# A four-layer mixer trunk on one core: fewer bias copies, norm rows two slots apart, spatial mixes in the other PSUM pool, first transfers reordered

## The chip, the cores and the metric

The program runs on one core of one Trainium2 chip. The metric is the device time of one execution in microseconds (us); the time before is the median of three runs. Four engines compute: TensorE (PE in the profile; its weight loads are PEld), VectorE (DVE), ScalarE (ACT) and GpSimd (POOL). SyncE (SP) only issues transfers here. Each engine works through its own queue in order, and an instruction that waits holds up everything behind it on that engine. Transfers (DMAs) are issued from the queues of SP, ACT and POOL and are carried out by 16 DMA engines that they share.

## What is computed

The reference is a trunk of four layers over 256 tokens of width 2048, in float32. Every layer normalises the stream, multiplies it by one wide input projection, runs a mixer over 1536 columns and an attention over 256 memory tokens over the other 512, gates the result and projects it back:

```python
mem_n = rms_norm(mem, mem_norm_g)
for i in range(4):
    h = rms_norm(x, norm_g[i])
    z = h @ w_in                      # mixer inputs | memory queries | gate
    # layers 0 and 3: gated spatial mixing, layer 1: forgetting attention,
    # layer 2: differential attention with a relative position bias
    mix_out = mixer(z[..., :n_mix])
    kv = mem_n @ w_mem_kv[i]
    mem_out = memory_attention(rms_norm(z_q), rms_norm(kv[..., :512]), kv[..., 512:])
    x = x + (concatenate([mix_out, mem_out]) * silu(gate)) @ w_out[i]
```

Two parts matter for the change. The spatial mixing of layers 0 and 3 multiplies 128 tokens at a time by a 128 x 128 matrix for each of 12 channel groups. The differential attention of layer 2 adds to the scores of each of its 12 heads a bias that depends only on the distance of key and query: `bias = table[t5_bucket(kpos - qpos)]`. So a row of 383 numbers per head holds all of it, and each query's row of 256 is a window of that row, one place further along than the next query's.

## The kernel before

**Products in slots.** All weights, some 300 MB, are read once from device memory, in pieces of 512 KB (128 partitions x 1024 float32). A piece is one slot: SP loads it into a `raw` buffer (line 105), ACT rounds it into `whi` (line 118), DVE subtracts to get the rest `wlo` (line 119), and PE does 12 matmuls of 128x512 with it, three products for each of two halves and two token tiles (lines 185 to 187). The three products together stand for one product in more exact arithmetic. Eight slots make a chunk of 512 output columns. There are 592 slots. Four `raw` buffers and four pairs `whi`/`wlo` let the splitting run up to four slots ahead of PE, and the loads up to eight.

**Tasks between slots.** The order of PE, ACT, DVE and SP is written out by hand. Everything that is not a slot is a Python generator, a task. Before each slot every live task runs up to its next `yield` (a tick), then the splits and loads for later slots are emitted, then what tasks put off (`late`). So a `yield` more moves a task's rest one slot back in all four queues, against the slots. A task that is spawned runs its first part at once, and its second part two ticks later. POOL's order is not written by hand: a planner places POOL's instructions, so that one can be placed well ahead of where the text of the program has it.

**The parts that the change touches.**

- The start (lines 251 to 277): the gains `gk`, the first piece of the transposed memory (`raw`, tile `xraw`) and the first weights (`w_raw`) are loaded in halves from the queues of ACT and SP, and ten matmuls on zeros run meanwhile.
- `token_rms` (line 295) loads 256 token rows in four column blocks of two tiles each (line 308), lets ACT square and sum them two steps later (line 301), and at its end computes the factors `r_mem` or `r_x`. Its tiles come from a rotation of six buffers, tag `mo`. It runs twice: for the memory from the seventh tick on during the first 16 slots, and for `x` during the keys of the last memory projection. One step takes one tick.
- `norm_task` (line 377) normalises queries or keys of a chunk: squares on ACT, sums on DVE, a power on POOL (line 335, reads DVE's sums), scaling on DVE (line 349), a byte shuffle on ACT (line 359) and two DMA transposes on SP (line 364), a join on DVE (line 369), a gain on ACT (line 393), then `done()`, for which the attention waits.
- `gmlp_mix_task` (line 717) is the spatial mix; its result `sv` is a PSUM tile of pool `ps_s` (line 730). `ps_s` has two buffers and also serves the scores `s` of all attentions (line 509); `ps_t`, two buffers too, serves the attentions' transposes and products `tb` (line 595).
- `diff_setup` (line 469) computes the 12 bias rows on PE near the end of layer 0 and writes them to device memory (`bias_d`) in 128 copies, with a pitch of 513, in eight writes of 16 copies each (line 492, on POOL's queue). `bias_load` (line 496) reads the bias of four heads into SBUF with a single transfer of 128 partitions, each from another copy (line 502, POOL's queue). With that pitch a partition finds its shifted window at a constant step of 512. Layer 2 loads three such biases into a rotation of two buffers: two at its start, the third when the first chunk's attention has ended.

In layers 0 to 2 `residual_task` (line 833) adds the output chunk to the stream, stores it (`x_d`, POOL's queue), squares it, turns it with two DMA transposes (`xq`, line 364, by way of the helper `turn`), joins the halves on DVE (`wide`, line 369) and splits it for the next layer.

Of the kernel before, what the change touches and what calls it, by code (L numbers as in the profile page):

```python
# [20 lines left out]
P = 128  # L21
D = 2048
S = 256
# [7 lines left out]
BIG = 3.0e38  # L31
BIAS_PITCH = 512
RAW_BUFS = 4
PART_BUFS = 4
# [8 lines left out]
def trunk_kernel(  # L43
# [213 lines left out]
    bparts[0] = (m_hi, m_lo)  # L257
    nc.scalar.dma_start(gk, gk_in)
    nc.scalar.dma_start(raw[:, :S], mem_t[0, :, :S])
    nc.sync.dma_start(w_raw[:, :CW], pieces[0][0][0, :, :CW])  # L260
    nc.sync.dma_start(raw[:, S:], mem_t[0, :, S:])
    nc.sync.dma_start(w_raw[:, CW:], pieces[0][0][0, :, CW:])
# [32 lines left out]
    def token_rms(src, r):  # L295
        ss = small.tile([P, 2, 4], F32, tag="ss", name="ss", bufs=2)
        rows = {}
        for n in range(6):
            if n >= 2:
                for t, row in enumerate(rows.pop(n - 2)):  # L300
                    nc.scalar.activation(
                        row, row, AF.Square, accum_out=ss[:, t, n - 2 : n - 1]
                    )
            if n < 4:
                rows[n] = []
                for t in range(2):
                    row = tmp.tile([P, CW], F32, tag="mo", name="row", bufs=6)
                    nc.sync.dma_start(
                        row, src[t * P : (t + 1) * P, n * CW : (n + 1) * CW]
                    )  # L310
                    rows[n].append(row)
            if n < 5:
                yield
        late.append(lambda: finish_rms(ss, r))
# [62 lines left out]
    def norm_task(acc, rcols, gain, width, dst, done=None):  # L377
# [15 lines left out]
        nc.scalar.activation(dst, dst, AF.Copy, scale=gain)  # L393
        yield
        if done:
            done()
# [18 lines left out]
    spawn(load_transposed(mem_t, "b", 4 * KT, bparts, early, 1, 2))  # L415
    spawn(delayed(6, token_rms(mem, r_mem)))
    first_accs = pair_product(lambda kp: bparts[kp])
# [46 lines left out]
    nc.gpsimd.dma_start(onehot, onehot_in)  # L464
    bias_row = P * (BIAS_PITCH + 1)
    bias_d = dram.tile([NH, bias_row], F32, name="bias_d")


    def diff_setup():
# [14 lines left out]
        bd = bias_d[:, :]  # L484
        for a in range(0, P, 16):
            for _ in range(4):
                yield
            rows = bass.AP(
                tensor=bd.tensor, offset=bd.offset + a * (BIAS_PITCH + 1),
                ap=[[bias_row, NH], [BIAS_PITCH + 1, 16], [1, 384]],  # L490
            )
            nc.gpsimd.dma_start(
                rows, onehot[:NH].unsqueeze(1).to_broadcast([NH, 16, 384])
            )

    def bias_load(dst, c):
        bd = bias_d[:, :]
        src = bass.AP(
            tensor=bd.tensor, offset=bd.offset + 4 * c * bias_row + P - 1,
            ap=[[BIAS_PITCH, P], [bias_row, 4], [1, S]],  # L500
        )
        nc.gpsimd.dma_start(dst, src)

# [213 lines left out]
    def gmlp_mix_task(acc, rcols, v, ws, c, j, mos, flag):  # L717
# [11 lines left out]
        for t in range(2):  # L729
            sv = ps_s.tile([P, CW], F32, tag="s", name="sv")  # L730
            mo = tmp.tile([P, CW], F32, tag="mo", name="mo", bufs=6)
# [148 lines left out]
    for i in range(DEPTH):  # L880
# [65 lines left out]
        else:  # L946
# [3 lines left out]
            if kind == 1:  # L950
                cq = act.tile([P, 2, NH], F32, tag="cq", name="cq")
            else:
                for c in range(2):
                    bias_load(biases[c], c)
                fflag.append(True)
            width = HD if kind == 1 else HD // 2
            gq, gkc = (G_BQ, G_BK) if kind == 1 else (G_CQ, G_CK)
            for c in range(3):
# [18 lines left out]
                def finish(mo, c=c):  # L977
                    mos[c] = mo
                    if c == 0:
                        biases[2] = new_bias()  # L980
                        (cum_load if kind == 1 else bias_load)(biases[2], 2)

# [114 lines left out]
```

## Time and profile before

| | |
|---|---|
| runs | median 1751.71 us, 1748.94 to 1752.92 (3 runs) |
| profiled execution | 1753.51 us, its span from first to last instruction 1751.7 us |
| busy share of the span | PE 99%, DVE 61%, ACT 56%, POOL 7% |
| moved | 381.13 MB, mean 218 GB/s |
| mean granted TensorE clock | 0.997 |

The span is cut into views: the waits list who waited for whom in total, the windows give busy time and the number of instructions (x) of each engine in a stretch, with the granted clock (PEclk, 1.00 is full) and the share of DMA engine time in use; the timeline has each instruction's start, duration, engine, line and in brackets how long its engine sat idle before it and what ended that. A busy share of 99% does not say that PE runs at its full rate: ends of matmuls are modelled and a matmul's time counts as busy however slowly the next one follows. The number of matmuls in a window says more.

### The profile page before, as it was taken

How to read it: one execution, taken by the hardware profiler on the slowest of the kernel's cores; microseconds unless marked ns; L12 is line 12 of the kernel's file. 1: busy time of each engine (PE TensorE's matmuls, PEld its weight loads, DVE VectorE, ACT ScalarE, POOL GpSimd, SP SyncE). 2: the span in 40 equal slices, each digit the busy share in tenths (PEclk: the TensorE clock that was granted, in tenths of full speed). 3: DMA queues.
4: the chain of work that ended last, by engine and by line, in shares of the span. 5: the costliest groups of instructions: out<-in, count | busy, mean ns of one | idle time of the engine just before them, and what ended most of it. 6: DMA issues, size and time to landing. Idle time of an engine off the chain costs nothing.

```text
span 1751.7 us, 21860 instructions
## 1 busy us (share of the span) xinstructions
PE 1733.1 (99%) x7918; PEld 1424.9 (81%) x7918; DVE 1075.2 (61%) x1539; ACT 981.6 (56%) x1347; POOL 124.5 (7%) x142
## 2 busy tenths in 40 slices
PE   9999999999999999999999999999999999999999
PEld 7888787888778888888888888878888888888887
DVE  5656557565556656666666666767576656755553
ACT  6555645555555655565655665665575554555542
POOL 1111101000000100000000101101000000100000
PEclk9999999999999999999999999999999999999999
DMA  8888867577898666676688776666668887656774
GB/s 299 270 248 269 264 224 209 166 214 178 244 254 265 187 181 213 193 201 207 190 252 256 240 193 203 183 182 196 196 182 251 263 244 231 181 174 197 205 237 161
DMA packets 207260, 381.13 MB, mean 218 GB/s; under 512 B 113796, under 2 KB 116240, under 8 KB 207152
## 3 DMA queue, kind: packets, MB, share of 16 engines
q1 hardware_dynamic: 199440, 358.01, 68.6%
q0 software_dynamic: 6272, 20.50, 4.2%
q8 instruction: 62, 1.02, 0.2%
q10 hardware_dynamic: 1440, 1.22, 0.2%
q14 instruction: 46, 0.38, 0.1%
HBM read 339.55 MB, written 14.95 MB: 202 GB/s over the span
## 4 chain that ended last, share of the span: by engine, by line
PE 90%; DMA 6%; ACT 2%; DVE 1%; issue 1%; SPq 0%; POOL 0%; ACTq 0%; DVEq 0%; POOLq 0%
PE acc L185 28%; PE acc L186 28%; PE acc L187 28%; PE tb L602 2%; DMA raw<-in_w_o_dram 1%; ACT whi L118 1%; DMA xraw<-in_mem_t_dram 1%; PE tb L611 1%; DMA sq<-pl 1%; DVE wlo L119 1%; DMA xraw<-in_x_t_dram 1%; PE s L510 1%; PE s L552 1%; DMA xq<-pl 1%; PE sv L734 1%
## 5 line engine op out<-in xcount | busy, mean ns | idle before, releaser
L119 DVE TENSOR_TENSOR wlo<-raw,whi 128x1024 fp32r<-128x1024 f32 x591 | 719.3, 1223 | 487.3 <-ACT whi L118 482.4
L118 ACT CAST whi<-raw 128x1024 fp32r<-128x1024 f32 x591 | 616.6, 1050 | 460.5 <-PE acc L187 339.2
L185 PE MATMUL acc<-whi,xh 128*128 128x512 f32 x1600 | 637.3, 398 | 0.0
L187 PE MATMUL acc<-whi,xl 128*128 128x512 f32 x1600 | 623.9, 390 | 0.0
L186 PE MATMUL acc<-wlo,xh 128*128 128x512 f32 x1600 | 623.6, 390 | 0.0
L185 PEld LDWEIGHTS acc<-whi,xh 128*128 128x128 f32 x1600 | 300.5, 188 | 67.3 <-issue 4.2
L187 PEld LDWEIGHTS acc<-whi,xl 128*128 128x128 f32 x1600 | 300.3, 188 | 63.8
L186 PEld LDWEIGHTS acc<-wlo,xh 128*128 128x128 f32 x1600 | 300.7, 188 | 59.8
L185 PE MATMUL acc<-whi,bh 128*128 128x512 f32 x764 | 299.7, 392 | 7.3 <-ACT whi L118 5.9
L186 PE MATMUL acc<-wlo,bh 128*128 128x512 f32 x764 | 299.9, 393 | 3.5 <-DVE wlo L119 3.3
L187 PE MATMUL acc<-whi,bl 128*128 128x512 f32 x764 | 299.0, 391 | 0.0
L185 PEld LDWEIGHTS acc<-whi,bh 128*128 128x128 f32 x764 | 144.4, 189 | 39.4 <-ACT whi L118 6.7
L186 PEld LDWEIGHTS acc<-wlo,bh 128*128 128x128 f32 x764 | 144.4, 189 | 37.2 <-DVE wlo L119 6.8
L187 PEld LDWEIGHTS acc<-whi,bl 128*128 128x128 f32 x764 | 144.3, 189 | 30.1 <-DVE bl L221 0.2
L615 ACT COPY pt<-tb 128x256 f32<-128x256 f32 (+1 forms) x80 | 27.3, 341 | 126.9 <-PE tb L611 126.9
L335 POOL TENSOR_TENSOR sc<-sc,expo 128x8 f32<-128x8 f32 (+1 forms) x23 | 58.3, 2533 | 426.0 <-DVE sc L334 265.2
L359 ACT COPY pl<-sq 128x1024 uint16<-128x1024 uint16 x40 | 39.8, 1043 | 5.8 <-DVE sq L349 5.7
L220 ACT ACTIVATE xh<-wide,gk 128x256 fp32r<-128x256 f32 x48 | 20.5, 498 | 39.6 <-DVE wide L369 39.6
L369 DVE COPY wide<-xq 128x1024 uint16<-128x1024 uint16 x24 | 18.1, 754 | 36.7 <-DMA xq<-pl 36.2
L848 POOL DMA_DIRECT2D x_d<-xo x24 | 13.3, 554 | 326.6 <-DVE xo L847 326.1
L359 ACT COPY pl<-mo 128x1024 uint16<-128x1024 uint16 x32 | 31.9, 1044 | 7.7 <-DVE mo L658 7.6
L515 DVE TENSOR_REDUCE st<-s 128x1 f32<-128x256 f32 x32 | 13.5, 421 | 30.4 <-PE s L510 30.3
(170 smaller groups left out, 994.5 us busy)
## 6 DMA issues: line engine op xcount, KB each, us to landing
raw<-in_w_a_dram SPq DMA_DIRECT2D x176, 512.0 KB, 4.3
raw<-in_w_o_dram SPq DMA_DIRECT2D x128, 512.0 KB, 4.4
raw<-in_w_b_dram SPq DMA_DIRECT2D x112, 512.0 KB, 4.2
raw<-in_w_c_dram SPq DMA_DIRECT2D x112, 512.0 KB, 4.1
raw<-in_w_kv_dram SPq DMA_DIRECT2D x63, 512.0 KB, 4.9
x_d<-xo POOLq DMA_DIRECT2D x24, 256.0 KB, 6.1
xo<-x_d SPq DMA_DIRECT2D x24, 256.0 KB, 5.7
lnp<-in_ln_dram SPq DMA_DIRECT2D x12, 256.0 KB, 6.0
```

The source lines that it names most:

```text
L118: nc.scalar.copy(hi, raw)
L119: nc.vector.tensor_sub(lo, raw, hi.bitcast(F32))
L185: nc.tensor.matmul(acc[t], xh[:, c], wh, start=begin, stop=False)
L186: nc.tensor.matmul(acc[t], xh[:, c], wl, start=False, stop=False)
L187: nc.tensor.matmul(acc[t], xl[:, c], wh, start=False, stop=end)
L220: nc.scalar.activation(hi, src, AF.Copy, scale=g)
L335: nc.gpsimd.tensor_tensor(sc[:, :, :n], sc[:, :, :n], expo.rearrange("p (a b) -> p a b", a=2)[:, :, :n], ALU.pow,)
L359: nc.scalar.copy(pl.rearrange("p (h e) -> p h e", h=2), src.bitcast(U16).rearrange("p (e h) -> p h e", h=2),)
L369: nc.vector.tensor_copy(wide[:, :, t, :].bitcast(U16).rearrange("p c (r h) -> p h c r", h=2), tts[t].rearrange("p (h c) r -> p h c r", h=2),)
L510: nc.tensor.matmul(s[:, :S], qt[:, h, t * P : (t + 1) * P], mk[:, h * S : (h + 1) * S], start=True, stop=True,)
L602: nc.tensor.matmul(av, pt[:, j * P : (j + 1) * P], vv[:, j, f], start=(j == 0), stop=(j == tiles(t) - 1),)
L615: nc.scalar.copy(pt[:, : nk * P], tb[:, : nk * P])
```

## The change

Five edits are made together.

- **First transfers.** The gains are loaded in two parts: the memory's part (the last 16 columns) on SP behind the first half of the weights, the rest on ACT behind the first half of the memory piece, which is now first on ACT.
- **Norm rows.** `token_rms` yields twice after each step; for the memory it starts three ticks earlier (delay 3, was 6).
- **`norm_task`** yields once more between the gain and `done()`.
- **Spatial mixes.** `sv` is allocated in `ps_t`.
- **Bias.** 16 copies are written in a single transfer instead of 128 in eight. A load reads 16 partitions at a time, eight transfers of 64 KB instead of one of 512 KB, one issued per tick. The two loads at the start of layer 2 become tasks delayed by 1 and 10 ticks, the third a task too.

```diff
+BIAS_COPIES = 16
...
-    nc.scalar.dma_start(gk, gk_in)
     nc.scalar.dma_start(raw[:, :S], mem_t[0, :, :S])
     nc.sync.dma_start(w_raw[:, :CW], pieces[0][0][0, :, :CW])
+    nc.sync.dma_start(gk[:, 4 * KT :], gk_in[:, 4 * KT :])
+    nc.scalar.dma_start(gk[:, : 4 * KT], gk_in[:, : 4 * KT])
     nc.sync.dma_start(raw[:, S:], mem_t[0, :, S:])
...
             if n < 5:
                 yield
+                yield
         late.append(lambda: finish_rms(ss, r))
...
         nc.scalar.activation(dst, dst, AF.Copy, scale=gain)
         yield
+        yield
         if done:
             done()
...
-    spawn(delayed(6, token_rms(mem, r_mem)))
+    spawn(delayed(3, token_rms(mem, r_mem)))
...
-    bias_row = P * (BIAS_PITCH + 1)
+    bias_row = BIAS_COPIES * (BIAS_PITCH + 1)
...
-        for a in range(0, P, 16):
-            for _ in range(4):
-                yield
-            rows = bass.AP(
-                tensor=bd.tensor, offset=bd.offset + a * (BIAS_PITCH + 1),
-                ap=[[bias_row, NH], [BIAS_PITCH + 1, 16], [1, 384]],
-            )
-            nc.gpsimd.dma_start(
-                rows, onehot[:NH].unsqueeze(1).to_broadcast([NH, 16, 384])
-            )
+        rows = bass.AP(
+            tensor=bd.tensor, offset=bd.offset,
+            ap=[[bias_row, NH], [BIAS_PITCH + 1, BIAS_COPIES], [1, 384]],
+        )
+        nc.gpsimd.dma_start(
+            rows, onehot[:NH].unsqueeze(1).to_broadcast([NH, BIAS_COPIES, 384])
+        )
+        yield

     def bias_load(dst, c):
         bd = bias_d[:, :]
-        src = bass.AP(
-            tensor=bd.tensor, offset=bd.offset + 4 * c * bias_row + P - 1,
-            ap=[[BIAS_PITCH, P], [bias_row, 4], [1, S]],
-        )
-        nc.gpsimd.dma_start(dst, src)
+        for p in range(0, P, BIAS_COPIES):
+            src = bass.AP(
+                tensor=bd.tensor, offset=bd.offset + 4 * c * bias_row + P - 1 - p,
+                ap=[[BIAS_PITCH, BIAS_COPIES], [bias_row, 4], [1, S]],
+            )
+            nc.gpsimd.dma_start(dst[p : p + BIAS_COPIES], src)
+            yield
...
-            sv = ps_s.tile([P, CW], F32, tag="s", name="sv")
+            sv = ps_t.tile([P, CW], F32, tag="t", name="sv")
...
-                for c in range(2):
-                    bias_load(biases[c], c)
+                spawn(delayed(1, bias_load(biases[0], 0)))
+                spawn(delayed(10, bias_load(biases[1], 1)))
                 fflag.append(True)
...
-                        (cum_load if kind == 1 else bias_load)(biases[2], 2)
+                        if kind == 1:
+                            cum_load(biases[2], 2)
+                        else:
+                            spawn(bias_load(biases[2], 2))
```

## The prediction, made before the changed kernel was run

> **What bounds the kernel now.** I read the page's busy times first, then what PE waited for, then a window around each wait, beside a window with none.
>
> ```profile
> PE 1733.1 (99%) x7918; PEld 1424.9 (81%) x7918; DVE 1075.2 (61%) x1539; ACT 981.6 (56%) x1347; POOL 124.5 (7%) x142
> ```
>
> PE is the bound: its matmuls are fixed in number and the change leaves them all in place. Only time in which PE halts or runs slowly can be won, and only new halts can cost. The waits of PE:
>
> ```profile
> PE acc L185 <- ACT whi L118: 5.9, 2, 3.8
> PE acc L186 <- DVE wlo L119: 3.3, 5, 1.5
> PE sv L734 <- ACT p L518: 1.8, 2, 1.0
> PE acc L185 <- ACT bh L220: 0.6, 1, 0.6
> PE s L510 <- ACT mqt L393: 0.5, 1, 0.5
> ```
>
> Columns: total us, times, longest. There are few halts, so each can be priced by itself. The windows (stretch, length, busy and number of instructions by engine, granted clock, DMA share, GB/s):
>
> ```profile
> 60.00:80.00 20.00, 20.00 (x90) 16.55 (x89) 11.46 (x12) 11.22 (x13) 3.21 (x5) 1.00 0.87 262
> 40.00:50.00 10.00, 9.41 (x40) 7.01 (x39) 6.33 (x11) 8.13 (x15) 0.73 (x1) 1.00 0.76 264
> 170.00:190.00 20.00, 17.14 (x68) 13.46 (x67) 7.69 (x11) 13.31 (x25) 1.63 (x1) 0.91 0.79 292
> 440.00:460.00 20.00, 15.79 (x57) 12.16 (x56) 6.12 (x7) 9.60 (x11) 0.00 (x0) 0.83 0.88 261
> 480.00:500.00 20.00, 18.52 (x81) 14.83 (x81) 12.19 (x15) 7.73 (x11) 0.35 (x1) 1.00 0.95 235
> 500.00:520.00 20.00, 19.65 (x86) 15.77 (x86) 11.14 (x13) 12.70 (x18) 2.00 (x4) 1.00 0.94 279
> 525.00:545.00 20.00, 20.00 (x90) 16.56 (x89) 13.61 (x16) 11.54 (x18) 1.08 (x2) 1.00 0.94 280
> ```
>
> Undisturbed, 20 us hold 90 matmuls, 0.222 us each; a slot of 12 is 2.67 us. The disturbed windows hold fewer: 22 missing at 170 to 190 (4.9 us), 33 at 440 to 460 (7.3 us), 9 and 4 at 480 to 520 (2.9 us), 5 of 45 at 40 to 50 (1.1 us). In the second and third of these the granted clock is below 1.00: after the halt PE runs slowly for a while. That part is in the counts, so a halt avoided returns it too.
>
> **Bias write: 7.3 us and 2.9 us.** What made the halt at 445?
>
> ```profile
> 424.44 3.07 POOL L492 DMA_DIRECT2D bias_d<-onehot  x5 [86.24 <-DVE onehot L483]
> 426.93 20.99 DMA raw<-in_w_o_dram
> 404.00:424.00 20.00, 20.00 (x88) 15.76 (x87) 11.58 (x18) 12.73 (x15) 0.00 (x0) 1.00 0.80 220
> 430.00:436.00 6.00, 6.00 (x28) 4.97 (x27) 2.79 (x6) 1.05 (x1) 0.00 (x0) 1.00 0.97 148
> 448.02 1.04 ACT L118 CAST whi<-raw 128x1024 fp32r<-128x1024 f32 x1 [9.44 <-DMA raw<-in_w_o_dram]
> raw<-in_w_o_dram SPq DMA_DIRECT2D x128, 512.0 KB, 4.4
> bias_d<-onehot POOLq DMA_DIRECT2D x8, 288.0 KB, 12.1
> ```
>
> The eight writes are four ticks apart in the program, yet POOL issues five within 3.07 us: a `yield` orders the hand-written queues, and POOL waits for data alone. The writes fill the DMA engines (share 0.97) while little moves (148 GB/s against 220 before). A weight piece that lands in 4.4 us as a rule takes 20.99, ACT idles 9.44 us for it, PE runs out of split weights. After the change there is one such write. Of the 16.6 us by which the piece was late, PE's lookahead covered 16.6 - 7.3 = 9.3. A fifth of the burst delays by a fifth, 3.3 us (an estimate from these rows), well under 9.3: nothing of it reaches PE. I take the whole 7.3. The other bound is that a fifth of it stays, 1.5.
>
> The last three writes stand in POOL's queue behind the stores of layer 0's output and meet the transposes of the stream:
>
> ```profile
> 476.23 1.25 POOL L492 DMA_DIRECT2D bias_d<-onehot  x2
> 477.82 10.83 SPq L364 DMA_TRANSPOSE xq<-pl  x2
> 489.76 0.75 DVE L369 COPY wide<-xq 128x1024 uint16<-128x1024 uint16 x1 [7.39 <-DMA xq<-pl]
> 911.76 4.92 SPq L364 DMA_TRANSPOSE xq<-pl  x2
> ```
>
> Two transposes occupy SP for 10.83 us beside the writes, and for 4.92 us in layer 1, where nothing is written. DVE waits 7.39 us for them with `wlo` queued behind, and PE waits for `wlo`. Without the writes I expect layer 1's picture: 2.9 us. That the stage's other traffic alone does it (nothing gained) is the bound; against it stands 525 to 545, same stage, no bias write, share 0.94 too, and all 90 matmuls.
>
> **Norm rows of x: 4.9 us.**
>
> ```profile
> 166.24 8.66 DMA row<-in_x_dram
> 174.93 0.63 ACT L301 ACTIVATE row<-row 128x512 f32<-128x512 f32 x1 [7.30 <-DMA row<-in_x_dram]
> 177.25 0.50 PE L185 MATMUL acc<-whi,bh 128*128 128x512 f32 x1 [2.10 <-ACT whi L118]
> ```
>
> ACT reaches the first square 7.30 us before its rows land, and every later cast stands behind it. The first block is now squared at the fifth tick after its load instead of the third (a spawned task loses one tick at its start). So two more casts and subtractions come ahead of the wait, weights for 2 x 2.67 = 5.3 us of PE, where PE stood for 2.10 us and then some 0.9 (`wlo`); the rest of the 4.9 is the slow clock after. The halt goes. SP's queue gains nothing that it could wait for: rows 2 find free buffers, rows 3 those of rows 0, squared two ticks before. `r_x` is complete at tick 11 instead of 6 and first used after tick 16.
>
> **Norm rows of the memory: 0.6 us.**
>
> ```profile
> 40.41 0.42 SPq L232 DMA_DIRECT2D xraw<-in_mem_t_dram  x1
> 46.17 0.91 ACT L220 ACTIVATE bh<-xraw,gk 128x256 fp32r<-128x256 f32 x2 [1.20 <-DMA xraw<-in_mem_t_dram]
> 25.00:30.00 5.00, 5.00 (x23) 4.13 (x22) 4.68 (x6) 2.88 (x5) 0.00 (x0) 1.00 0.67 209
> ```
>
> The last memory piece is issued late, behind the rows in SP's queue, and PE waits for its `bh`. The rows now start at tick 4 instead of 7, into a stretch with free DMA time (0.67), and no square waits for its load, so SP and ACT should reach that piece some us sooner. But rows 2 and 3 still wait on SP for squares in their own tick. Bounds 0 and 1.1; I take the middle. `r_mem` is complete two ticks later, at tick 14 of 16, ahead of its use.
>
> **Spatial mixes and the tick in `norm_task`: 2.3 us.** `sv` waits 1.8 us (layers 0 and 3) because its `ps_s` buffer is held by the scores of the first attention unit until ACT's exponential. In `ps_t` its buffer has been free for many slots, and the first `tb` comes a tick after the second `sv`, into the buffer of the first, which DVE has read by then. If that cover failed, `tb` would wait about what `sv` waited, 1.0 us each. The tick lets PE reach the first score a slot (2.67 us) later, where it waited 0.5. It costs a tick only where the attention already waits: memory attentions end a slot later, their results are used many slots later; for the mixers' own keys the eight slots of the value chunk cover it. The last gates don't move.
>
> **First transfers: 0.**
>
> ```profile
> 1.18 0.46 ACTq L259 DMA_DIRECT2D xraw<-in_mem_t_dram  x1
> 5.09 0.51 ACT L220 ACTIVATE bh<-xraw,gk 128x256 fp32r<-128x256 f32 x1 [1.94 <-DMA xraw<-in_mem_t_dram]
> 10.74 1.05 ACT L118 CAST whi<-raw 128x1024 fp32r<-128x1024 f32 x1 [1.38 <-DMA raw<-in_w_kv_dram]
> 10.00:15.00 5.00, 4.77 (x20) 3.63 (x21) 3.08 (x5) 3.01 (x3) 0.00 (x0) 1.00 1.00 379
> ```
>
> The first memory half goes out 0.44 us earlier (0.74, ACT's first issue) and the gains reach SP's queue at 1.2, so the first product may start 0.3 us sooner. But the third weight piece is waited for anyway, at 10.74, from DMA engines in full use (1.00), and everything on SP behind the gains is issued some 0.4 later. I take nothing, between 0.4 lost and 0.4 won.
>
> **Bias loads: 0.** 24 transfers stand for 3, on POOL:
>
> ```profile
> 747.14 0.81 POOL L502 DMA_DIRECT2D bias<-bias_d  x1 [42.25 <-DVE lg L532]
> 796.20 2.55 POOL L335 TENSOR_TENSOR sc<-sc,expo 128x8 f32<-128x8 f32 x1 [18.16 <-DVE sc L334]
> 842.05 0.80 POOL L502 DMA_DIRECT2D bias<-bias_d  x1 [42.25 <-DVE lg L532]
> 1119.98 0.82 POOL L502 DMA_DIRECT2D bias<-bias_d  x1 [17.38 <-DVE mo L623]
> 1126.52 2.93 POOL L335 TENSOR_TENSOR sc<-sc,expo 128x16 f32<-128x16 f32 x1 [5.72 <-DVE st L574]
> L644 DVE MEMSET bias<- x3: 272/272/272, 1072.9 to 1245.6; 64x256 f32 x3
> ```
>
> The first two are issued long before layer 2, as soon as layer 1 frees a buffer. With eight issues of at most 0.82 us each takes 6.6 us instead of 0.82. First use is at 1072.9 and the third chunk's at 1245.6, over 100 us after the issue. POOL has no power to compute for tens of us around 747 and 842; after 1119.98 the eight issues end at 1126.5, just when the next power (1126.52) starts. Three slots (8.0 us) lie between a power and its use.
>
> The Trainium skill speaks against more transfers from this queue: SBUF — State Buffer, section "SBUF: two separate sides", says that descriptors of a POOL-issued DMA can't be written while DVE holds the shared port in a two-port copy, and gives 620 ns alone against about 3100 beside such a copy. DVE's joins (0.75 us) are copies; no POOL issue in the rows above shows it, the longest being 0.82. By that figure the third bias would hold POOL for 24.8 us (an estimate from that page) and, less the 10.7 of cover in rival 3 and two slots of lookahead, add 8.8: 1742.5.
>
> **The sum.** 7.3 + 2.9 + 4.9 + 0.6 + 2.3 = 18.0 us. The profiled execution takes 1753.5, its span 1751.7; less 18.0 that is 1735.5 and 1733.7. The runs' median, 1751.71, is 1.8 below the execution and by chance the span; the forecast for the median is 1751.7 - 18.0 = 1733.7.
>
> **Rivals.**
>
> 1. The stall moves on: with PE ahead, the loads of the residual stage set the pace. A fifth of the burst's halt stays (1.5), the transposes stay late (2.9), the memory rows give nothing (0.6): 1733.7 + 5.0 = 1738.7. For it: DMA share 0.94 there. Against: the 90 matmuls at that same share.
> 2. The rows of x are late all the same, since ACT catches up with the two casts faster than the rows land: 1733.7 + 4.9 = 1738.6. For: 7.30 us of wait, two casts take 2.1. Against: those casts feed PE longer than it stood.
> 3. POOL's issues cost more. From 1.3 us each, (6.5 + 4.2) / 8 with 6.5 us to the next power and 4.2 left of the 8.0 after a power and its two products, the scaling on DVE is late and `wlo` behind it. At twice the longest row (1.64) it is 2.4 us late, which PE's lookahead of about two slots hides; at three times, 9.0 late, some 4 reach PE: 1738. The rule above is this case carried further.
> 4. Slower than before: the planner puts one of the sixteen early pieces ahead of the power at 796.20 in POOL's queue. That piece can't go before 842.05, so the power comes 46 us late, the scaling and all `wlo` behind it too; less the lookahead of four slots (10.7) PE stands about 35: 1733.7 + 35 = 1769. It decides as soon as a single piece is so placed. For: sixteen pieces instead of two, all placed by the planner. Against: their place in the program is layer 2, and both loads of before went behind the powers that were due.
> 5. The change doesn't do what it says: the halts are partly the profiled execution's own (the lowest run, 1748.94, is 4.6 below it), and half of the 18.0 is there to win: 1742.7.
>
> **How the numbers follow.** Forecast 60 in 100, rival 1 15, rival 2 8, rival 3 6, rival 4 4, rival 5 7. The forecast's own range is 1731 (the start's 0.4, the memory rows' other 0.5, and a rest of the 0.2 and 0.5 us halts) to 1736.5 (the fifth that stays, no gain from the memory rows, 0.4 lost at the start). Cases 1 to 3 reach to 1739, case 5 to 1742.7. I give 1730 to 1742. About what a measurement can tell from no change is 0.2%, 3.5 us: faster means below 1748.2. All cases but the fourth are there, less a share for rivals not thought of: faster 0.92, same 0.04, slower 0.04.
>
> **What would show it.** Right: 90 matmuls in the 20 us from the bias write on, at full clock, and a weight piece landing in under 8 us there; transposes of layer 0's stream near 5 us; no PE wait at the rows of x; `sv` and the first score without a wait. Wrong: a clock below 1.00 after the start; a power on POOL whose sums are long done; PE waiting for `whi` or `wlo` at a place that had no wait before. The forecast fails as a whole if the halts return elsewhere with the same total.

## The result, and the profile after

The changed kernel takes 1736.94 us, the median of four runs (1736.56 to 1738.77), against 1750.43 us for four runs of the kernel before (1748.94 to 1752.92): the ratio is 0.992, 95% interval 0.9903 to 0.9936. A second set of its runs, beside other kernels (below), gave 1737.32 against 1751.46, 0.9917 (0.9903 to 0.9932). Its profiled execution took 1737.19 us, span 1735.4, where that of before took 1753.51 and 1751.7. The forecast was 1733.7, within 1730 to 1742.

PE's line of the page and PE's waits, after (total us, times, longest):

```profile
PE 1726.9 (100%) x7918; PEld 1423.2 (82%) x7918; DVE 1076.3 (62%) x1539; ACT 985.9 (57%) x1349; POOL 129.0 (7%) x156
...
PE acc L186 <- ACT mvv L404: 1.7, 1, 1.7
PE acc L187 <- DVE wlo L120: 1.2, 2, 0.8
...
PE acc L186 <- ACT whi L119: 0.5, 1, 0.5
```

Of the longest items of before, `whi` is down from 5.9 to 0.5 us, `wlo` from 3.3 to 1.2, and `sv` (1.8) is gone. One line is new: PE waits 1.7 us for `mvv`. Where the time went is seen best by counting matmuls stage by stage. The windows of the kernel before:

```profile
0.00:16.00 16.00, 13.49 (x48) 8.27 (x49) 7.76 (x12) 9.28 (x15) 4.48 (x14) 1.00 0.87 297
16.00:65.00 49.00, 48.41 (x212) 39.06 (x210) 28.43 (x37) 30.03 (x49) 3.91 (x6) 1.00 0.86 287
65.00:190.00 125.00, 122.14 (x531) 100.28 (x530) 70.74 (x83) 72.74 (x98) 12.40 (x14) 0.99 0.84 260
190.00:430.00 240.00, 238.47 (x1096) 197.64 (x1095) 148.23 (x198) 127.53 (x152) 15.40 (x16) 1.00 0.70 209
430.00:480.00 50.00, 45.78 (x189) 37.00 (x188) 23.59 (x28) 24.04 (x28) 2.42 (x4) 0.93 0.89 222
480.00:530.00 50.00, 48.16 (x210) 38.88 (x210) 29.39 (x34) 27.54 (x38) 3.43 (x6) 1.00 0.95 268
530.00:1600.00 1070.00, 1069.21 (x4973) 881.11 (x4972) 687.53 (x1062) 624.98 (x902) 82.48 (x82) 1.00 0.71 210
```

and the same windows after:

```profile
0.00:16.00 16.00, 13.12 (x42) 7.50 (x43) 6.94 (x11) 8.38 (x12) 4.46 (x14) 1.00 0.83 271
16.00:65.00 49.00, 47.30 (x207) 38.09 (x206) 28.63 (x36) 30.27 (x51) 4.86 (x6) 1.00 0.87 284
65.00:190.00 125.00, 125.00 (x553) 103.50 (x552) 73.26 (x85) 74.11 (x97) 10.59 (x13) 1.00 0.85 270
190.00:430.00 240.00, 240.00 (x1106) 199.56 (x1106) 149.30 (x202) 130.14 (x158) 13.05 (x13) 1.00 0.71 212
430.00:480.00 50.00, 50.00 (x222) 41.43 (x221) 29.94 (x33) 29.52 (x36) 1.66 (x3) 1.00 0.80 239
480.00:530.00 50.00, 50.00 (x223) 41.38 (x222) 32.37 (x37) 29.24 (x43) 3.23 (x6) 1.00 0.91 266
530.00:1600.00 1070.00, 1070.00 (x4978) 882.27 (x4977) 686.00 (x1057) 626.71 (x899) 91.12 (x101) 1.00 0.71 209
```

The differences in PE's counts, at 0.222 us each:

| stretch | matmuls | us | forecast |
|---|---|---|---|
| 0 to 16, the start | -6 | -1.3 | 0 |
| 16 to 65, memory rows and first `mvv` | -5 | -1.1 | +0.6 |
| 65 to 190, rows of x | +22 | +4.9 | +4.9 |
| 190 to 430, spatial mixes of layer 0 | +10 | +2.2 | about half of 2.3 |
| 430 to 480, bias write burst | +33 | +7.3 | +7.3 |
| 480 to 530, transposes | +13 | +2.9 | +2.9 |
| 530 to 1600, with the mixes of layer 3 | +5 | +1.1 | the other half |

Together 72 matmuls or 16.0 us, against 16.3 between the two spans. From 65 us on the forecast holds almost term by term, 18.4 us won where 17.4 was forecast. The first 65 us lose 2.4 where 0.6 was to be won. The starts of the slots, counted along PE's timeline, say the same: slot 3 starts at 15.73 before and 17.03 after, slot 20 at 63.41 and 65.78.

What the bias did on the queue of POOL, and how long the weight pieces took to land beside the write (the timeline of POOL; the raw pieces from 420 to 432, shortest, median, longest; the first two transposes of the stream on SP):

```profile
419.65 0.64 POOL L493 DMA_DIRECT2D bias_d<-onehot  x1 [83.53 <-DVE onehot L487]
...
DMA to landing us min/median/max: 3.8/6.0/7.4
...
465.62 5.58 SPq L367 DMA_TRANSPOSE xq<-pl  x2
```

The pieces take at most 7.4 us, where one took 20.99 before. The first two transposes take 5.58 us instead of 10.83, the next two 5.56 instead of 7.89.

The loads of the bias, POOL's timeline:

```profile
732.27 4.12 POOL L505 DMA_DIRECT2D bias<-bias_d  x8 [42.25 <-DVE lg L536]
759.59 2.58 POOL L338 TENSOR_TENSOR sc<-sc,expo 128x8 f32<-128x8 f32 x1 [23.19 <-DVE sc L337]
...
1105.12 2.61 POOL L505 DMA_DIRECT2D bias<-bias_d  x5 [17.39 <-DVE mo L627]
1111.66 2.92 POOL L338 TENSOR_TENSOR sc<-sc,expo 128x16 f32<-128x16 f32 x1 [3.93 <-DVE st L578]
1114.54 0.54 POOL L505 DMA_DIRECT2D bias<-bias_d  x1
```

Eight issues take 4.12 us, at a point where POOL had been idle for 42 us. The third load was split around a power: five pieces before it, three behind.

The new loss lies in the first stage. SP's first issues and ACT's cast of the third weight piece, after:

```profile
3.08 0.43 SPq L233 DMA_DIRECT2D xraw<-in_mem_t_dram  x1
4.16 0.81 SPq L106 DMA_DIRECT2D raw<-in_w_kv_dram  x2
...
12.01 1.05 ACT L119 CAST whi<-raw 128x1024 fp32r<-128x1024 f32 x1 [2.65 <-DMA raw<-in_w_kv_dram]
```

and the same in the kernel before, whose cast of that piece at 10.74 stands in the prediction:

```profile
2.61 0.43 SPq L232 DMA_DIRECT2D xraw<-in_mem_t_dram  x1
3.08 1.64 SPq L105 DMA_DIRECT2D raw<-in_w_kv_dram  x2
```

In both kernels SP issues six transfers 0.47 us apart and then pauses ahead of the seventh: after, 3.08 + 0.43 = 3.51 to 4.16; before, the pause lies inside the row of two issues, 1.64 us for what otherwise takes 0.81. The list of SP's waits in the first 6 us names what it waits for, before and after:

```profile
SPq L105 <- DMA gk<-in_gk_dram: 0.9, 1, 0.9
...
SPq L106 <- DMA xraw<-in_mem_t_dram: 0.6, 1, 0.6
```

Both are the first transfer on ACT's queue. It lands at 4.38 before and at 4.14 after, and the paused issue goes out at 4.40 and 4.16. By the trace's records the two transfers use the same semaphore, the counter that tells of a landing. Two transfers on ACT and six on SP go out without such a wait; the ninth of the two queues together waits. The third weight piece was the eighth in that count before. With the gains split in two and one part ahead of it on SP it is the ninth, goes out 1.08 us later, and is cast 1.27 us later.

Then, around 50 us, timelines of ACT, POOL and PE after:

```profile
46.67 0.91 ACT L221 ACTIVATE bh<-xraw,gk 128x256 fp32r<-128x256 f32 x2 [1.54 <-DMA xraw<-in_mem_t_dram]
...
48.43 0.63 ACT L303 ACTIVATE row<-row 128x512 f32<-128x512 f32 x1
...
52.32 1.64 POOL L291 TENSOR_TENSOR r_mem<-r_mem,expo 128x2 f32<-128x2 f32 x1 [46.85 <-DVE r_mem L290]
...
54.00 1.27 ACT L404 ACTIVATE mvv<-acc,r_mem 128x512 f32<-128x512 f32 x2 [1.40 <-POOL r_mem L291]
...
54.74 0.50 PE L186 MATMUL acc<-whi,bh 128*128 128x512 f32 x1 [1.70 <-ACT mvv L404]
```

The last squares of the memory rows run at 48.43, behind the split of the last memory piece, which itself waited for its load. `r_mem` is ready at 53.97; `mvv`, the first reader of the product, needs it, and PE needs the PSUM tile that `mvv` reads.

### The profile page after: what moved, and what is told of

Read it like the earlier page. It is cut to its first block, busy times and chain, and to the rows that moved or that the text cites. A ratio compares the mean times of both kernels' runs of the same rounds, so it can differ in the third digit from the quotient of the medians.

```text
span 1735.4 us, 21890 instructions
## 1 busy us (share of the span) xinstructions
PE 1726.9 (100%) x7918; PEld 1423.2 (82%) x7918; DVE 1076.3 (62%) x1539; ACT 985.9 (57%) x1349; POOL 129.0 (7%) x156
## 4 chain that ended last, share of the span: by engine, by line
PE 97%; DMA 2%; ACT 1%; DVE 0%; SPq 0%; issue 0%; POOL 0%; DVEq 0%; ACTq 0%
PE acc L186 31%; PE acc L187 30%; PE acc L188 30%; PE tb L606 2%; DMA xraw<-in_mem_t_dram 1%; PE tb L615 1%; PE s L514 1%; PE s L556 1%; DMA raw<-in_w_kv_dram 1%; PE sv L738 1%; PE s L531 0%; ACT whi L119 0%; DVE wlo L120 0%; PE acc L158 0%; ACT row L303 0%
## 5 line engine op out<-in xcount | busy, mean ns | idle before, releaser
L519 DVE TENSOR_REDUCE st<-s 128x1 f32<-128x256 f32 x32 | 13.5, 422 | 31.3 <-PE s L514 31.3
```

## The experiments

"The kernel before" in a measurement is always the one that ran on the same chip. Slot starts are those of one profiled execution.

**The first stage: which edit costs what.** Two suspects stand in the traces: the start (the third piece in seventh place on SP) and the late `r_mem`. They may be two losses, each with its own price, or both may only feed one loss, so that undoing one moves the wait elsewhere.

The old order of the first transfers in the changed kernel:

```diff
-    nc.scalar.dma_start(raw[:, :S], mem_t[0, :, :S])
-    nc.sync.dma_start(w_raw[:, :CW], pieces[0][0][0, :, :CW])
-    nc.sync.dma_start(gk[:, 4 * KT :], gk_in[:, 4 * KT :])
-    nc.scalar.dma_start(gk[:, : 4 * KT], gk_in[:, : 4 * KT])
+    nc.scalar.dma_start(gk, gk_in)
+    nc.scalar.dma_start(raw[:, :S], mem_t[0, :, :S])
+    nc.sync.dma_start(w_raw[:, :CW], pieces[0][0][0, :, :CW])
```

> The changed kernel with the first transfers of before (all gains on ACT's queue ahead of the memory piece). Theory A, place in SP's queue: in the changed kernel the gains make the third weight piece the seventh transfer on SP, issued at 4.16 us instead of 3.08, and ACT gets it at 12.0 instead of 10.7; so here the cast of the third piece is back near 10.7, the fourth slot starts near 15.7 instead of 17.0, and 1.3 us are won, some 1735.5 us. Theory B, the DMA engines set the landing whatever the order (share 0.98 to 1.01 from 5 to 15 us in both): the third piece still comes near 12, and the time stays at 1736.9.

The memory's gains on ACT, right behind the memory piece, so that SP's queue is as before:

```diff
-    nc.sync.dma_start(gk[:, 4 * KT :], gk_in[:, 4 * KT :])
+    nc.scalar.dma_start(gk[:, 4 * KT :], gk_in[:, 4 * KT :])
```

> The changed kernel with both parts of the gains on ACT's queue behind the memory piece; SP's queue has no gains. Theory A, place in SP's queue: as with the old start the third weight piece is cast near 10.7, and the first product still starts near 5.5 to 6; 1735.2 to 1735.5 us. If instead the order on ACT's queue made the loss, nothing is won here and the old start alone wins it. Theory B: third piece near 12, 1736.9.

The memory rows as before (one slot apart, delay 6), the rows of x two apart:

```diff
-    def token_rms(src, r):
+    def token_rms(src, r, pace=2):
...
-                yield
-                yield
+                for _ in range(pace):
+                    yield
...
-    spawn(delayed(3, token_rms(mem, r_mem)))
+    spawn(delayed(6, token_rms(mem, r_mem, 1)))
```

> The changed kernel with the memory's rows at the pace of before (delay 6, one tick a step); the rows of x keep two ticks. Theory: the wait of PE for the mvv activation at 52.6 us (1.86 lost) is the late r_mem, so it goes; the wait for the last memory piece near 46 us (1.0 lost in the kernel before) comes back: about 0.8 us won, 1736.1. The wait at the rows of x stays away. Rival: the 52.6 wait comes from the start being 1.3 us later, not from the rows' pace; then it stays and the other comes back too, 1737.9.

The memory rows two apart, but two ticks earlier:

```diff
-    spawn(delayed(3, token_rms(mem, r_mem)))
+    spawn(delayed(1, token_rms(mem, r_mem)))
```

> The changed kernel with the memory's rows two ticks earlier still (delay 1, two ticks a step), so that the last squares are at tick 12. Theory: r_mem is complete some 5 us earlier and the wait for mvv goes; the last memory piece still comes in time: 1.8 us won, 1735.1. Rival: the first rows now go into the stretch where the DMA engines are full (0.91 to 1.01 up to 20 us) and delay weight pieces: PE waits there for up to the 512 KB that two steps of rows move, 1.6 us at 300 GB/s, and nothing is won.

The changed kernel once more, as it is, beside the next ones:

> The changed kernel once more, as the reference for the runs beside it. If its first stage repeats, slot 20 starts near 65.8 us again, with waits for wlo or whi of the second and third slots and a wait for mvv. If its scatter is as wide as that of the four variants seen (65.1 to 67.1), any value between 64.5 and 67 may come.

Both undone, the old start and the old memory rows (the first and third diff above):

> The changed kernel with the first transfers and the memory's rows of before, so that its first 20 slots are those of the kernel before. Theory: these two edits cost what the first stage lost; slot 20 starts near 63.4 us as in the kernel before, 2.4 us earlier than in the changed kernel, 1734.5. Rival: the first stage scatters by 1 to 2 us whatever is in it; slot 20 near 65 to 66 and the time no different from the changed kernel beside it.

Measured (times in us; third piece: start of its cast on ACT; the kernel before on the same chip: 1750.43 beside the first profile, 1753.10 beside the four variants below it, 1751.46 beside the next two):

| kernel | median, lowest to highest | third piece | slot 3 | slot 20 | PE's wait for `mvv` |
|---|---|---|---|---|---|
| changed, first profile | 1736.94, 1736.56 to 1738.77 | 12.01 | 17.03 | 65.78 | 1.7 |
| old start | 1736.49, 1736.41 to 1737.15 | 11.36 | 16.33 | 65.09 | 1.7 |
| gains on ACT | 1737.65, 1736.17 to 1738.47 | 11.26 | 16.21 | 67.11 | 1.7 |
| memory rows as before | 1736.25, 1735.23 to 1737.52 | 11.77 | 16.76 | 66.01 | none |
| memory rows earlier | 1737.11, 1736.18 to 1739.52 | 11.52 | 16.50 | 65.26 | none |
| changed, again | 1737.32, 1735.98 to 1738.95 | 11.60 | 16.58 | 66.94 | 1.7 |
| both as before | 1735.42, 1734.88 to 1736.26 | 10.49 | 15.48 | 63.50 | none |
| the kernel before | | 10.74 | 15.73 | 63.41 | none |

The kernel before alone differs by 2.7 us from chip to chip in this table, and the ranges of the single variants overlap that of the changed kernel, so the medians don't tell the single variants apart; the starts of the slots, one execution each, have to. The old start alone brings slot 3 to 16.33, where 15.7 was expected. Three things follow. The two edits are the whole loss of the first stage: with both undone slot 20 starts where it did before (63.50 and 63.41). Three executions of kernels further below agree: slot 20 starts at 62.78 and 63.45 in two that leave the first stage as it was before, and at 66.00 in one that has both edits. The two edits don't add: undone singly they bring slot 20 to 65.1 and 66.0 from 65.8 to 66.9, little more than the two executions of the changed kernel differ by, and undone together to 63.5. And a wait removed from PE's list is no gain by itself: with the old memory rows the 1.7 us for `mvv` is gone, but PE's waits there read

```profile
PE acc L187 <- DVE wlo L120: 2.1, 3, 0.8
...
PE acc L186 <- ACT bh L221: 0.5, 1, 0.5
```

where the first profile of the changed kernel has 1.2 for `wlo` and no `bh`; its second profile has 1.3 for `bh` too, at 37.09 us. With the rows earlier the 1.7 us is gone as well, and slot 20 is only 0.5 us sooner than in the first profile, where 1.8 was expected: PE waits 1.4 us for `bh`. So the second reading is nearer.

The gains on ACT tell what the start costs. SP's queue is as before there and the third piece is in sixth place again, and yet it doesn't go out at 3.08 as in the kernel before:

```profile
4.06 0.82 SPq L106 DMA_DIRECT2D raw<-in_w_kv_dram  x2
...
SPq L106 <- DMA xraw<-in_mem_t_dram: 0.9, 1, 0.9
```

With three transfers on ACT it is still the ninth of both queues, and it waits for ACT's first landing (4.04). So the expectation, place in SP's queue, was not the right count: moving the gains to the other queue doesn't take the wait away. The piece is cast 0.34 us sooner than in the second profile of the changed kernel, and slot 20 starts as late (67.11 and 66.94). Nothing behind the first stage takes part: between 65 and 1600 us PE begins 7073 matmuls in the changed kernel, and 7073, 7073, 7072, 7073 and 7073 in these five variants (in the order of the table; 7070 in the changed kernel's second profile). What slot 20 loses in these, the end loses.

**What holds the first stage.** In the changed kernel's chain of waits the same round turns again and again:

```profile
17.81 4.93 DMA xraw<-in_mem_t_dram
22.92 0.27 issue
23.19 0.49 ACT bh L221
23.68 0.95 ACT whi L119
24.66 1.24 DVE wlo L120
25.91 0.33 SPq L106
...
27.71 7.09 DMA xraw<-in_mem_t_dram
```

A memory piece lands, ACT splits it, then casts the weights queued behind; DVE's subtraction frees a `raw` buffer; only then can SP issue the weight load that waits for that buffer, and the next memory piece stands behind it in SP's queue, to land 5 to 7 us later. If this round is the bound, then issuing each memory piece one step earlier breaks it, whatever the start and the rows do. If the bytes are the bound, it doesn't, but fewer bytes would. (The tiles of tag `mo` get eight buffers instead of six for it.)

```diff
-            if kp < KT // 2:
-                raws_t[kp] = transposed_load(src, kp)
+            while loaded < min(kp + ahead + 1, KT // 2):
+                raws_t[loaded] = transposed_load(src, loaded)
+                loaded += 1
...
-    spawn(load_transposed(mem_t, "b", 4 * KT, bparts, early, 1, 2))
+    spawn(load_transposed(mem_t, "b", 4 * KT, bparts, early, 1, 2, 1))
```

> The changed kernel with the transposed memory pieces loaded one step (two slots) earlier, two in flight instead of one, and eight mo buffers instead of six. Theory, a loop of latencies: ACT waits 1.5 to 3.6 us for every memory piece (period 5.6 to 6.3 us for two slots, where PE needs 5.4), because the piece is issued only when the piece before it has been split; here these waits go, r_mem comes in time, slot 20 starts near 63 us, 2 to 2.5 us are won. Rival, the amount of data: the DMA engines are full (0.91 to 1.01) and the pieces only move the waits to the weights; slot 20 stays at 65 to 66.

Only the first quarter of each memory row's columns loaded and squared, so that three quarters of the sum behind `r_mem` are left out:

```diff
-                        row, src[t * P : (t + 1) * P, n * CW : (n + 1) * CW]
+                        row[:, :cols], src[t * P : (t + 1) * P, n * CW : n * CW + cols]
...
-    spawn(delayed(3, token_rms(mem, r_mem)))
+    spawn(delayed(3, token_rms(mem, r_mem, CW // 4)))
```

> The changed kernel with the memory's rows cut to a quarter: only 128 of each 512 columns are loaded and squared, so 1.5 MB and three quarters of the sum behind r_mem are left out. If the amount of data sets the first stage, 1.5 MB at 300 GB/s is 5 us of DMA time less: the waits for the memory pieces go and slot 20 starts at 63 us or earlier. If the loop of latencies sets it, the pieces still come some 6 us apart and slot 20 stays within 1 us of 65.8; the wait for mvv may shorten by what the shorter squares save on ACT (under 1 us).

Pieces one step ahead: 1735.12 us (1734.57 to 1735.61) beside 1737.32 (1735.98 to 1738.95) for the changed kernel on the same chip, no run of the one among those of the other. Slot 3 is as late as ever (17.07), and yet slot 20 starts at 63.31. ACT no longer waits for a memory piece; it waits for weights instead, and for PE to hand back `whi` buffers:

```profile
23.30 1.05 ACT L119 CAST whi<-raw 128x1024 fp32r<-128x1024 f32 x1 [2.04 <-DMA raw<-in_w_kv_dram]
...
47.20 1.05 ACT L119 CAST whi<-raw 128x1024 fp32r<-128x1024 f32 x1 [1.67 <-PE acc L188]
...
50.87 1.26 ACT L406 ACTIVATE mvv<-acc,r_mem 128x512 f32<-128x512 f32 x2
```

`mvv` runs at 50.87 instead of 54.00, without a wait, with the rows still two slots apart. So the round is a bound of its own. Of the 2.5 us by which slot 20 is earlier than in the first profile of the changed kernel, 1.6 reach the end: between 145 and 157 us, where the pieces of `x` are split in the same way, 0.9 are lost, with a wait of PE for `wlo` at 151.37 that the changed kernel's first profile doesn't have. A quarter of the rows: 1735.77 us in a single execution, slot 20 at 63.19, no wait of PE for `mvv`, though ACT still waits for memory pieces (4.31, 0.72, 4.05 and 3.44 us). If the bytes were the bound, slot 20 at 63 was expected and these waits were to go; only the first came. So less work for the rows helps as much by another way. It takes away ACT's time and DMA's bytes at once, and which of the two did it stays open.

With the first stage no longer bound by that round, the start should count again. Pieces ahead and the old start together:

> The changed kernel with the first transfers of before and the memory pieces loaded one step earlier (eight mo buffers). If the two gains add, the fourth slot starts near 15.7 us (old start) and nothing waits for memory pieces or r_mem after it: slot 20 near 62 us, some 3.5 us less than the changed kernel, 1733.5. If the DMA engines set the first stage from here on, the earlier pieces only push the weights back: slot 20 near 63.3 as with either alone, 1735.1.

1733.56 us (1733.14 to 1734.23) against 1751.96 for the kernel before on that chip, ratio 0.9893 (0.9874 to 0.9912). Slot 3 starts at 15.53 and slot 20 at 61.77; against the pieces ahead alone that is 1.5 us each, so in this pair of executions the start carries through in full. No run of the changed kernel was under 1735.98, and none of this version over 1734.23. It was run on another chip than the changed kernel, but the kernel before takes the same there within 0.5 us (1751.96 and 1751.46). So this version is faster than both kernels. PE's waits in it, all but one of 0.2 us:

```profile
PE warm_ps L270 <- DVE warm L267: 1.2, 1, 1.2
PE acc L186 <- ACT whi L274: 0.9, 1, 0.9
PE acc L187 <- DVE wlo L120: 0.4, 1, 0.4
```

**The burst.** Was it the five writes at once, as predicted, or simply the bytes written? In the kernel before, all eight writes stay, but go out on SP's queue, whose order the ticks do set:

```diff
-            nc.gpsimd.dma_start(
+            nc.sync.dma_start(
                 rows, onehot[:NH].unsqueeze(1).to_broadcast([NH, 16, 384])
             )
```

> The kernel before with one difference: its eight bias writes are issued from SP's queue, where the four ticks between them hold, instead of POOL's. The bytes are the same 2.36 MB. Theory, the burst: one write delays a weight piece by 3.3 us, the lookahead covers it, so the halt at 445 us (7.2 lost between slots 150 and 166) goes; the last writes still meet the transposes of layer 0's stream, so up to 1 us each may be lost there. Between slots 150 and 180, where the kernel before takes 91.7 us and the changed one 81.6, 82 to 85. Rival, the amount: the same packets cost the same DMA time wherever they are, and the loss only spreads: 88 to 92.

1743.76 us in a single execution. The writes went out from 432.76 to 512.76, 8 to 15 us apart. The windows around them:

```profile
430.00:460.00 30.00, 30.00 (x134) 24.78 (x132) 13.51 (x13) 15.61 (x17) 0.54 (x1) 1.00 0.84 213
460.00:520.00 60.00, 58.22 (x257) 47.93 (x256) 37.84 (x43) 35.48 (x50) 3.25 (x6) 1.00 0.97 282
```

All the bytes of before, and of the 7.3 us nothing is lost up to 460, at full clock. Ten matmuls (2.2 us) go in the 60 us after, when DMA is in use at 0.97 and two transposes take 6.99 us. Slots 150 to 180 take 83.7 us, against 91.7 before and 81.6 after, inside the expected band. With the same bytes spread out, most of the time is back. The writes have changed their queue too; whether a bunch on SP's queue would cost as much was not run.

And how does it grow? Four of the former writes at once, in the changed kernel:

```diff
-BIAS_COPIES = 16
+BIAS_COPIES = 64
...
+        for a in range(0, BIAS_COPIES, 16):
+            rows = bass.AP(
+                tensor=bd.tensor, offset=bd.offset + a * (BIAS_PITCH + 1),
+                ap=[[bias_row, NH], [BIAS_PITCH + 1, 16], [1, 384]],
+            )
+            nc.gpsimd.dma_start(
+                rows, onehot[:NH].unsqueeze(1).to_broadcast([NH, 16, 384])
+            )
+        yield
```

> The changed kernel with 64 copies, written in four writes issued at once (64 partitions still read 16 at a time). By the prediction's working, four writes delay the weight piece by 4/5 of 16.6 us, 13.3; the lookahead covers 9.3; PE loses 4.0 between slots 150 and 166, where the kernel before takes 50.9 us and the changed one 43.5: some 47.5. Rival, loss in proportion to the bytes (7.2 for five): 5.8, some 49.3. Rival, a threshold above four: 43.5. The transposes are not touched.

1740.86 us in the profiled execution, span 1739.1. Slots 150 to 166 take 46.6 us against 43.5 with one write and 50.9 in the kernel before, with five. That is 3.1 us lost, somewhat less than the 4.0 of the prediction's working (delay in proportion, 16.6 x 4/5 = 13.3, less 9.3 that the lookahead covers). A loss in proportion to the writes, 0.8 of 7.3, would have given 49.3, and none 43.5: so there is a cover, and one write stays under it. The longest weight piece from 420 to 436 us took 17.6 us to land, 13.2 more than the usual 4.4, so the delay was in proportion and the cover 10.1.

**The spatial mixes alone.** In the kernel before, only `sv` moves to `ps_t`:

```diff
-            sv = ps_s.tile([P, CW], F32, tag="s", name="sv")
+            sv = ps_t.tile([P, CW], F32, tag="t", name="sv")
```

> The kernel before with the spatial mix's result in the other PSUM pool and nothing else. Theory, each edit removes its own wait: the wait of PE for the exponential at sv (1.8 us, twice) goes, the wait for the query's gain (0.5) and what hangs on it stays. Between slots 103 and 117 the kernel before takes 51.15 us and the changed one 49.00; here 49.9 to 50.1. Rival, the wait moves on: the next score needs the ps_s buffer that the exponential still holds, and PE waits there instead: 51.1.

1748.23 us in a single execution. PE's waits:

```profile
PE acc L185 <- ACT whi L118: 4.4, 2, 3.5
PE acc L186 <- DVE wlo L119: 4.3, 7, 1.6
```

are still there, for the burst and the rows of x; those for `sv` and `s` have gone from the list, both, though the wait for `s` was expected to stay. Slots 103 to 117 of layer 0 take 49.29 us, against 51.15 before and 49.00 after; slots 511 to 525 of layer 3 take 49.03, against 50.09 and 49.01. So the pool alone gives 1.9 of the 2.2 us in layer 0 and all of the 1.1 in layer 3. The tick in `norm_task` is left with 0.3 at most; it wasn't run alone. The halt in layer 3 is not in every execution: the kernel with the spaced writes leaves `sv` in `ps_s` and takes 49.31 us for slots 511 to 525, without a wait for `sv`, while its layer 0 has both waits and takes 51.03.

**The rows of x.** No kernel changes them alone, but the one with both first-stage edits undone differs from the kernel before, up to slot 70, only in these rows and in the tick of `norm_task`. Slots 56 to 70 take 43.10 us in the profile of before and 38.08 in that one, as in every other kernel with the rows two apart. In two kernels that keep them one apart, the one with spaced writes and the one with `sv` alone moved, these slots take 41.83 and 41.01. So the halt is worth 5.0 us in one execution and 3.8 and 2.9 in others.

## Why the prediction was right, and where it was wrong

The sign, the size and the range were right. The halts that were priced went, and from 65 us on none came back elsewhere; what came in their place is a loss in the first 65 us. The forecast was 3.2 us too low. The first 65 us account for 3.0 of that (2.4 lost where 0.6 was to be won) and the median for 1.8, as said below; the mixes, 1.0 better than forecast, took part of it back. The forecast's own narrower range, 1731 to 1736.5, was missed by 0.4; the parts named for it add up only to 1732.1 and 1736.2.

**Bias write, 7.3 us:** right, 33 matmuls or 7.3 us. Spreading the writes removed the halt with every byte still written, and four at once brought part of it back; the loss with four was 0.9 below what a cover of 9.3 us leaves.

**Last writes against transposes, 2.9 us:** right, 13 matmuls, and the transposes take 5.58 and 5.56 us, near those of layer 1 in the same execution (5.26 and 5.57).

**Rows of x, 4.9 us:** right, 22 matmuls between the two profiled executions. After the change ACT's wait at the first square is 0.51 instead of 7.30 us, behind waits for weights that PE doesn't notice. That the profile of before had this halt at its longest of three is chance.

**Memory rows, 0.6 us:** wrong, the stretch lost 1.1. The half that was priced came true in the first profile, where PE's wait for `bh` (0.6) is gone; in the second PE waits 1.3 us for another piece. The step that failed is the sentence that `r_mem` is complete "two ticks later, at tick 14 of 16, ahead of its use". I counted ticks, as if they had a length. ACT runs its ticks only when the memory pieces land, and at 46.67 it still waited for the last of them, with the last squares queued behind it. From there the rest of ACT's work, DVE, the power (1.64 us) and `mvv` end 1.7 us too late for PE. The trace of before had the row for it, quoted for another purpose: ACT waiting 1.20 us for that piece at 46.17.

**Spatial mixes and the tick, 2.3 us:** the mechanism was right and the size too small: 3.3 us (2.2 in layer 0, 1.1 in layer 3), of which `sv` alone accounts for 3.0. I summed the waits listed for `sv` and `s`, 1.8 + 0.5. What these waits cost in slots is more than the list shows for them; the counts of matmuls, used for the other terms, would have told.

**First transfers, 0 within 0.4:** wrong. The step that failed is "the third weight piece is waited for anyway [...] I take nothing". It is waited for, so what delays it is paid. And I priced an added issue on SP at one issue time, 0.4. The added transfer made the third piece the ninth of the two queues, which waits for ACT's first landing, and it went out 1.08 later; the row of before with two issues in 1.64 us, and SP's wait of 0.9 for `gk` there, showed that this place pays more. The seven executions with the new start have slot 3 between 16.50 and 17.07 (mean 16.76), the six with the old one between 15.48 and 16.54 (mean 15.87; the gains on ACT are counted with neither): 0.9 us lost, though the first product starts 0.5 earlier (means 5.52 and 6.03; 0.7 in the first two profiles).

**Bias loads, 0:** right. The first reader of the bias is DVE at 1058.4, over 200 us behind the second load. Rival 3 needed issues from 1.3 us on. All 24 of them:

```profile
L505 POOL DMA_DIRECT2D bias<-bias_d x24: 512/516/584, 732.3 to 1116.9; - x24
```

0.51 to 0.58 us, less than the 0.81 of the larger ones. The Trainium skill's rule (SBUF — State Buffer, section "SBUF: two separate sides"), by which a transfer issued by POOL takes some 3100 ns beside a two-port copy of DVE because its descriptors can't be written, shows in none of these 24 issues, with DVE busy 62% of the span; these runs do not show whether any of them met such a copy.

**The rivals.** The stall did not move on to the residual stage (rival 1): 223 matmuls in the 50 us from 480, at a share of 0.91. No load went ahead of a power that it blocked (rival 4). Rival 5, halts that belong to the profiled execution, holds in part. Between the two profiled executions the gain is 16.3 us, between the medians 13.5 and 14.1. I made the sum against the profiled execution and then subtracted it from a median that was 1.8 lower. Subtracted from its own time it gives 1753.5 - 18.0 = 1735.5, 1.7 off. All runs of before together spread from 1748.42 to 1755.14, seven on one chip over 6.4 us, while four of the last version on that chip spread over 1.1. That fits halts which are not equally long in every execution, and two of them are seen to vary: that at the rows of x (5.0, 3.8 and 2.9 us) and that of the mixes in layer 3 (1.1 and 0.3).

## What to carry to other kernels

Price a halt by the matmuls missing from its stretch, not by the wait in the list: three terms priced so were right to 0.1 us between the two profiles, and the one summed from waits was a third too small. Such a price holds for the execution it was read from; where executions differ, subtract it from that execution's own time. When a step is moved by so many ticks, find out what a tick waits for in that stage; here the ticks lasted as long as the memory pieces took to land. Before a transfer is put ahead of others, look in the list of the queue's own waits for what the later ones wait for. And in a stage where several engines wait in a round, undoing one edit at a time shows little: look for the link of the round (here a load queued behind one that waits for a buffer) and cut that.

## What the runs showed of the hardware

At the start, the first eight transfers from ACT's and SP's queues go out less than half a microsecond apart on each queue, and the ninth goes out 0.02 us after ACT's first has landed, which is 3.2 to 3.6 us after that one's issue; the two use the same semaphore. It does so in all 13 executions whose traces have this landing, in seventh place on SP's queue in twelve and in sixth place in the one with three transfers on ACT. So it is not a pause of SP's queue, and for this wait a transfer counts the same on either queue.

Writes issued in a bunch on POOL's queue cost far more than the same writes spread out on SP's: a weight piece took 20.99 us to land beside five writes of 288 KB, at most 17.6 beside four and at most 7.4 beside one, and PE lost 7.3 us to the five at once but nothing in the 30 us in which the first two of the spaced ones went out.
